# Gate and up tiles as seven block products, and a new order in the state-space stage

## The chip, the cores and the metric

The kernel runs on one core of a Trainium2 chip. The metric is the device time of one execution in microseconds. TensorE (PE) multiplies matrices and loads their weights (PEld) beside it, VectorE (DVE), ScalarE (ACT) and GpSimd (POOL) do the elementwise work, and SyncE (SP) issues nearly all transfers. Each engine runs its instructions in the order in which they stand, and waits on semaphores for the others. Products are summed in PSUM, eight banks of 512 float32 columns on 128 partitions; everything else lies in SBUF.

## The reference

The model is a trunk of two layers on 512 tokens of width 1024. Layer 0 mixes tokens with a diagonal state-space model, a gated projection (GLU) and an output projection; layer 1 with stick-breaking attention of 16 heads. After each mixer comes a feed-forward block of hidden width 2816, and after each of the four parts a normalisation of the scaled input plus the part's output.

```python
def swiglu_ffn(x, w_gu, w_down):
    g, u = jnp.split(x @ w_gu, 2, axis=-1)
    return (jax.nn.silu(g) * u) @ w_down
...
    for i in range(DEPTH):
        ...
        h = layer_norm(DEEPNORM_ALPHA * h + mix, ln_mix_g[i], ln_mix_b[i])
        h = layer_norm(DEEPNORM_ALPHA * h + swiglu_ffn(h, ffn_w_gu[i], ffn_w_down[i]),
                       ln_ffn_g[i], ln_ffn_b[i])
```

## The kernel before

Every float32 operand of a large product is split into a rounded high part and a low part that holds the rest, and a product is three passes: high by high, low weights by high, high weights by low (`mm3`). x lies transposed in `xh` and `xl`, 8 blocks of 128 features by 512 tokens. A weight chunk is 128 x 1024: it is brought in by SP as `raw`, ACT copies its high part `wh`, and DVE (or POOL, where `l_eng` says so) subtracts to get `wl` (`Weights.pump`, lines 228 and 231). All such tiles come from one ring of 37 SBUF slots that are handed out in the order in which they came free, so a transfer can wait for the last reader of its slot.

The feed-forward block (`ffn`) has 22 tiles of 128 hidden features. A tile is one gate chunk and one up chunk, 8 blocks x 3 passes x 2 = 48 matmuls of 512 columns (`fm`, lines 292 to 294), then SiLU on ACT (L409), the product with up on DVE (L410), and the split of the result (L287, L288). Tiles 0 and 1 are made by `ffn_first` at the end of the mixer, first for tokens 0 to 255 and then for the rest, so that PE has work while the last two of four token tiles are normalised (`ln`, L332 to L345) and transposed (`tr`, L357). The down product follows: 22 chunks into all eight banks for the first 14, and the last 8 token tile by token tile (`tail`), so that normalisation can start early.

In both feed-forward blocks DVE works in the order in which the code is written, in the second one ACT too; elsewhere a scheduler orders the instructions. The state-space stage follows a string, `SSM_ORDER`: each letter is a piece of work for one of four blocks of groups (g, j, h and i make tables on DVE, t and T transpose, m, k and y are small matmuls, e is a table on POOL, r and s rotate and scan, z applies GELU, l splits its result, n fetches a Toeplitz matrix from a DRAM scratch by 16 transfers), `d9` is nine unused matmuls of two passes that keep PE's clock up, `u1` is one item of GLU work on finished blocks, `p` and `q` split the next weight chunk with POOL or DVE, `a` adds partial GLU sums on POOL. `GLU_FIRST` lists those items: a GLU tile and the quarters of its input features; what isn't listed follows behind the stage.

## Time and profile before

| | us |
|---|---|
| median of 3 runs | 1248.2 (1247.43 to 1248.39) |
| profiled execution | 1248.96 |
| its span | 1247.2 |
| PE busy | 1191.5 |
| DVE busy | 666.4 |
| ACT busy | 422.6 |
| POOL busy | 190.5 |

A row of a time line gives start, length, engine, line, operation, tiles and shapes, and in brackets the engine's idle time before it and what ended it. A row of instruction groups gives count, total busy time, mean length in ns, and the idle time before them with its causes. A window row gives length and then, engine by engine, busy time and number of instructions (PE, PEld, DVE, ACT, POOL), the clock that TensorE was granted, the share of the transfer engines in use, and GB/s. Matmuls overlap, so that a row's length is more than the time to the next row's start.

### The profile page before, as it was taken

What the parts mean: (1) busy time and instruction counts of PE and PEld (TensorE: products, weight loads), DVE (VectorE), ACT (ScalarE), POOL (GpSimd) and SP (SyncE); (2) the same over time, 40 slices, a digit from 0 to 9 for tenths busy, and PEclk for the clock granted to TensorE, in tenths of its full rate; (3) what the DMA queues carried; (4) which work ended last, traced back from release to release, by engine and by line L of the source; (5) the groups of instructions that cost most, each with busy time, mean ns of one, the idle gap of its engine ahead of it and who ended that gap; (6) DMA issues with size and microseconds to landing.
All of it is one profiled execution on the core that took longest, in us unless ns stands there. A gap on an engine that the chain in (4) does not pass through costs nothing.

```text
span 1247.2 us, 16906 instructions
## 1 busy us (share of the span) xinstructions
PE 1191.5 (96%) x6964; PEld 989.7 (79%) x6964; DVE 666.4 (53%) x1033; ACT 422.6 (34%) x601; POOL 190.5 (15%) x212
## 2 busy tenths in 40 slices
PE   3799999999999999999999999999999999999996
PEld 2577688898888888888887888878888888888885
DVE  8975666643323333234867787868433333333236
ACT  1355263142222222222246666653222223332200
POOL 6636302120000000001312222224200000000000
PEclk9899999999999999999999999999999999999998
DMA  5333453142222223442201122133322222234301
GB/s 192 111 94 92 144 195 112 37 149 69 85 85 85 85 84 106 148 136 84 85 7 63 52 68 62 58 101 122 133 85 85 85 85 85 69 117 152 102 17 51
DMA packets 44781, 117.66 MB, mean 94 GB/s; under 512 B 6816, under 2 KB 18080, under 8 KB 44576
## 3 DMA queue, kind: packets, MB, share of 16 engines
q1 hardware_dynamic: 44704, 116.59, 29.3%
q8 instruction: 54, 0.88, 0.3%
q14 instruction: 23, 0.19, 0.1%
HBM read 112.51 MB, written 4.06 MB: 93 GB/s over the span
## 4 chain that ended last, share of the span: by engine, by line
PE 83%; DVE 9%; ACT 3%; POOL 2%; issue 1%; DMA 1%; SPq 1%; DVEq 0%; POOLq 0%; ACTq 0%
PE psum L294 17%; PE psum L292 17%; PE psum L293 16%; PE psum L313 8%; PE psum L312 8%; PE psum L311 8%; PE psum L776 2%; DVE nb L1015 2%; PE psum L1037 1%; DVE h L466 1%; ACT wh L228 1%; DVE wl L231 1%; PE psum L1102 1%; PE psum L1053 1%; PE psum L687 1%
## 5 line engine op out<-in xcount | busy, mean ns | idle before, releaser
L292 PE MATMUL psum<-xh,wh 128*128 128x512 f32 (+1 forms) x1056 | 394.6, 374 | 0.8 <-ACT xh L287 0.8
L294 PE MATMUL psum<-xl,wh 128*128 128x512 f32 (+1 forms) x1056 | 393.6, 374 | 0.0
L293 PE MATMUL psum<-xh,wl 128*128 128x512 f32 (+1 forms) x1056 | 391.9, 372 | 0.0
L228 ACT ACTIVATE wh<-raw 128x1024 fp32r<-128x1024 f32 x188 | 194.5, 1055 | 228.4 <-PE psum L313 68.5
L231 DVE TENSOR_TENSOR wl<-raw,wh 128x1024 fp32r<-128x1024 f32 x158 | 196.7, 1274 | 131.7 <-ACT wh L228 103.8
L292 PEld LDWEIGHTS psum<-xh,wh 128*128 128x128 f32 x1056 | 198.4, 188 | 38.7 <-issue 3.0
L293 PEld LDWEIGHTS psum<-xh,wl 128*128 128x128 f32 x1056 | 198.4, 188 | 35.4
L294 PEld LDWEIGHTS psum<-xl,wh 128*128 128x128 f32 x1056 | 197.9, 188 | 33.5
L410 DVE TENSOR_TENSOR s<-s,psum 128x512 f32<-128x512 f32 x44 | 30.3, 688 | 278.9 <-PE psum L294 278.9
L231 POOL TENSOR_TENSOR wl<-raw,wh 128x1024 fp32r<-128x1024 f32 x30 | 74.1, 2485 | 512.6 <-DMA raw<-w_v 317.2
L313 PE MATMUL psum<-wh,hid 128*128 128x512 f32 x352 | 137.6, 391 | 0.0
L312 PE MATMUL psum<-wl,hid 128*128 128x512 f32 x352 | 137.4, 390 | 0.0
L311 PE MATMUL psum<-wh,hid 128*128 128x512 f32 x352 | 137.3, 390 | 0.0
L287 ACT ACTIVATE hid<-s 128x512 fp32r<-128x512 f32 x44 | 27.7, 629 | 172.4 <-DVE s L410 172.4
L313 PEld LDWEIGHTS psum<-wh,hid 128*128 128x128 f32 x352 | 66.1, 188 | 14.2
L312 PEld LDWEIGHTS psum<-wl,hid 128*128 128x128 f32 x352 | 66.1, 188 | 14.0
L311 PEld LDWEIGHTS psum<-wh,hid 128*128 128x128 f32 x352 | 66.1, 188 | 13.5
L1016 POOL TENSOR_TENSOR be<-be,nb 128x768 f32<-128x768 f32 (+1 forms) x24 | 49.5, 2062 | 98.2 <-DVE nb L1015 70.9
L1015 DVE TENSOR_TENSOR_SCAN nb<-nb,dm 128x384 f32<-128x384 f32 (+1 forms) x48 | 50.2, 1088 | 9.7 <-ACT nb L1010 6.9
L409 ACT ACTIVATE s<-psum 128x512 f32<-128x512 f32 x44 | 26.2, 596 | 76.9 <-PE psum L294 76.8
L288 DVE TENSOR_TENSOR hid<-s,hid 128x512 fp32r<-128x512 f32 x44 | 30.5, 693 | 31.9 <-ACT hid L287 31.9
L287 ACT ACTIVATE xh<-psum 128x512 fp32r<-128x512 f32 x24 | 14.0, 596 | 97.1 <-PE psum L357 93.7
(181 smaller groups left out, 1399.8 us busy)
## 6 DMA issues: line engine op xcount, KB each, us to landing
raw<-w_gu SPq DMA_DIRECT2D x88, 512.0 KB, 3.6
raw<-w_down SPq DMA_DIRECT2D x44, 512.0 KB, 3.6
raw<-w_glu SPq DMA_DIRECT2D x16, 512.0 KB, 4.5
raw<-w_qk SPq DMA_DIRECT2D x16, 512.0 KB, 3.6
raw<-w_out SPq DMA_DIRECT2D x8, 512.0 KB, 3.7
raw<-w_v SPq DMA_DIRECT2D x8, 512.0 KB, 3.6
raw<-w_o SPq DMA_DIRECT2D x8, 512.0 KB, 3.6
xres<-xs SPq DMA_DIRECT2D x4, 512.0 KB, 6.9
```

The source lines that it names most:

```text
L228: nc.scalar.activation(h, w, AF.Copy)
L231: (self.l_eng or nc.vector).tensor_tensor(out=l, in0=w, in1=h.bitcast(F32), op=SUB)
L287: self.nc.scalar.activation(h, src, AF.Copy)
L288: self.nc.vector.tensor_tensor(out=l, in0=src, in1=h.bitcast(F32), op=SUB)
L292: mm(out=out, lhsT=sh, rhs=mh, start=first, stop=False)
L293: mm(out=out, lhsT=sl, rhs=mh, start=False, stop=False)
L294: mm(out=out, lhsT=sh, rhs=ml, start=False, stop=last)
L311: mm(out=o, lhsT=sh[:, ts], rhs=hl[0][:, c], start=first, stop=False)
L312: mm(out=o, lhsT=sh[:, ts], rhs=hl[1][:, c], start=False, stop=False)
L313: mm(out=o, lhsT=sl[:, ts], rhs=hl[0][:, c], start=False, stop=last)
L1015: V.tensor_tensor_scan(nb[:, h], nb[:, h], dm[u], 0.0, MUL, ADD)
L1016: G_.tensor_tensor(out=be, in0=be, in1=nb, op=MUL)
```

## The change

From the third tile on, gate and up of one tile are taken as a 2 x 2 block product: rows gate and up, inner halves of 512 features, columns tokens 0 to 255 and 256 to 511. With G1, G2, U1, U2 as the weight blocks and X11, X12, X21, X22 as blocks of x (first index the feature half), seven products replace eight: G1 X11, G2 X21, S4 X22, U2 T4, S1 T1, S2 T2 and S3 T3, with S1 = U1 + U2, S2 = S1 - G1, S3 = G1 - U1, S4 = G2 - S2, and T1 = X12 - X11, T2 = X22 - T1, T3 = X22 - X12, T4 = X21 - T2. `split_pair` makes the sums S of the next tile in three steps between the products of the present one, s1 and s2 in PSUM banks 6 and 7, the two halves of `s` in SBUF, and splits everything; `pair` issues the products and adds them up; `x_forms` makes the four T once for each layer at the end of the mixer. The hidden tile stays whole in `hid` and is split later, in the down part (`take`). The first two down chunks are brought in and split within the last tile, and their products begin with the banks that this tile leaves free. Weights of such a tile come as two transfers together. At the end of the first feed-forward block two instead of three chunks are fetched ahead. In the state-space stage the order and the GLU items change (17 instead of 20 quarters in the stage), seven `d9` stand instead of two, and the second half of the first Toeplitz matrix is fetched through ACT's queue.

The core of the difference:

```diff
 GLU_FIRST, GLU_LAST = glu_items(
-    "30 50 10 40 60 20 51 41 31 001 112 212 7012 612")
+    "30 50 10 40 60 20 001 51 41 312 7012 612")
...
 SSM_ORDER = (
-    "x c0 e0 g0 j0 t0 h0 T0 b0 i0 m0 M0 k0 n0 d9 r0 d9 s0 B0 c1 p e1 y0 g1 z0 t1 j1 T1 m1 M1 h1 p l0 u1 i1 c2 e2 p "
-    "u1 k1 n1 r1 u1 p u1 u1 s1 g2 y1 t2 j2 z1 T2 m2 M2 h2 p u1 i2 c3 l1 p k2 n2 r2 u1 u1 u1 a p e3 s2 g3 y2 t3 j3 "
-    "z2 T3 m3 M3 h3 p u1 i3 p l2 k3 n3 r3 u1 u1 p s3 q y3 q w0 z3 a w4 l3 q q q"
+    "x c0 e0 g0 j0 t0 T0 d9 h0 b0 i0 m0 M0 k0 n0 d9 d9 r0 d9 d9 d9 d9 s0 B0 c1 p e1 y0 g1 t1 j1 T1 z0 m1 M1 h1 l0 "
+    "u1 i1 c2 p u1 k1 n1 p r1 u1 u1 u1 e2 s1 p g2 y1 j2 t2 T2 z1 m2 M2 h2 p i2 c3 k2 n2 u1 e3 r2 l1 p u1 u1 s2 y2 "
+    "g3 t3 j3 T3 z2 m3 M3 h3 i3 k3 p n3 u1 l2 r3 u1 s3 p q y3 q w0 z3 a w4 l3 q q q"
...
-            t = self.ring.get("raw", F32)
-            self.nc.sync.dma_start(out=t, in_=self.src[self.loaded])
+            src = self.src[self.loaded]
+            if self.loaded > self.split + 1 and any(isinstance(s, tuple) for s in self.src[self.split:self.loaded + 1]):
+                break
+            if isinstance(src, tuple):
+                if self.hold:
+                    break
+                t = [self.ring.get("raw", F32) for _ in src]
+                for a, b in zip(t, src):
+                    self.nc.sync.dma_start(out=a, in_=b)
+            else:
+                t = self.ring.get("raw", F32)
+                self.nc.sync.dma_start(out=t, in_=src)
             self.raw[self.loaded] = t
             self.loaded += 1
+    def split_pair(self, i, g, u):
...
+        s1, s2 = self.sums
+        gh, gl, bh, bl, c, sh, sl = tiles = [get("wf") for _ in range(7)]
+        a = [(gh[:, lo], gl[:, lo]), (gh[:, hi], gl[:, hi]), (sh[:, hi], sl[:, hi]), (bh[:, lo], bl[:, lo]),
+             (bh[:, hi], bl[:, hi]), (c[:, lo], c[:, hi]), (sh[:, lo], sl[:, lo])]
+        self.hl[i] = dict(tiles=tiles, a=a)
+        s = get("ws", F32)
+        tt(s[:, lo], g[:, lo], u[:, lo], SUB, G_)
+        nc.scalar.activation(gh, g, AF.Copy)
+        nc.scalar.activation(bh[:, lo], u[:, hi], AF.Copy)
+        tt(gl, g, f(gh), SUB, G_)
+        tt(bl[:, lo], u[:, hi], f(bh[:, lo]), SUB, G_)
+        yield
+        tt(s1, u[:, lo], u[:, hi], ADD)
+        tt(s2, s1, g[:, lo])
+        tt(s[:, hi], g[:, hi], s2)
+        nc.scalar.activation(bh[:, hi], s1, AF.Copy)
+        nc.scalar.activation(c[:, lo], s2, AF.Copy)
+        nc.scalar.activation(sh, s, AF.Copy)
+        tt(bl[:, hi], s1, f(bh[:, hi]))
+        tt(c[:, hi], s2, f(c[:, lo]))
+        yield
+        tt(sl, s, f(sh))
+        self.ring.put(g, u, s)
+        self.split += 1
+        self.load(i + 1)
+    def begin(self, i):
+        if i >= len(self.src) or not isinstance(self.src[i], tuple):
+            return iter(())
+        self.load(i)
+        return self.split_pair(i, *self.raw.pop(i))
...
-        self.c_gu[l] = [[ws.add(io["w_gu"][l, i, v]) for v in range(2)] for i in range(KF)]
+        self.c_gu[l] = [[ws.add(io["w_gu"][l, i, v]) for v in range(2)] for i in range(2)]
+        self.c_gu[l] += [ws.add((io["w_gu"][l, i, 0], io["w_gu"][l, i, 1])) for i in range(2, KF)]
...
+    def x_forms(self, t):
...
+        x1, x2 = k4(u[:, :512]), k4(u[:, 512:])
+        part = lambda i, src: self.split(self.xf[i][0][:, :, c], self.xf[i][1][:, :, c], src)
+        tt(x1, x(self.xh, ka), x(self.xl, ka), ADD)
+        tt(x2, x(self.xh, kb), x(self.xl, kb), ADD)
+        yield
+        tt(u1, p1, x1)
+        tt(p2, p2, u1)
+        tt(x1, p2, x1)
+        tt(x2, x2, p2)
+        yield
+        part(1, p2)
+        part(0, u1)
+        part(2, x1)
+        part(3, x2)
+        ring.put(u, v)
+    def pair(self, i, a, ahead):
...
+        x11, x21, x22 = x(slice(0, 4), lo), x(slice(4, 8), lo), x(slice(4, 8), hi)
+        t1, t2, t3, t4 = self.xf
+        a11, a12, s4, a22, s1, s2, s3 = a
+        two = lambda t: t.rearrange("p (a b) -> p a b", a=2)
+        cu, vy = self.cv[:, 0:S], self.cv[:, S:2 * S]
+        s = self.tmp.tile([128, S], F32, tag="s", name="s")
+        def product(b, w, x):
+            wh, wl = (t.rearrange("p (k m) -> p k m", k=4) for t in w)
+            for k in range(4):
+                self.mm3(P[:, b], wh[:, k], wl[:, k], x[0][:, k], x[1][:, k], k == 0, k == 3)
+        next(ahead, None)
+        product(0, a11, x11)
+        p1 = vy[:, lo]
+        nc.scalar.activation(p1, P[:, 0], AF.Copy)
+        product(2, a12, x21)
+        product(3, s2, t2)
+        tt(two(cu), p1.unsqueeze(1).to_broadcast([128, 2, 256]), P[:, 2:4])
+        nc.scalar.activation(s[:, lo], cu[:, lo], AF.Silu)
+        next(ahead, None)
+        product(4, s1, t1)
+        product(5, s3, t3)
+        tt(two(vy), two(cu)[:, 1:2].to_broadcast([128, 2, 256]), P[:, 4:6])
+        tt(P[:, 5], vy[:, lo], P[:, 5])
+        next(ahead, None)
+        product(2, s4, x22)
+        product(3, a22, t4)
+        tt(P[:, 2:4], two(vy), P[:, 2:4])
+        nc.scalar.activation(s[:, hi], P[:, 2], AF.Silu)
+        o = self.hidden(i)
+        tt(two(o), two(s), P[:, 3:6:2], MUL)
...
-            store(3)
+            if forms:
+                E = mybir.EngineType
+                f, g = self.x_forms(2), self.x_forms(3)
+                next(f)
+                next(g)
+                with self.tc.manual_schedule(engines={E.Activation, E.DVE}):
+                    next(f)
+                    self.tr(3)
+                    next(g)
+                    for h in (f, g):
+                        for _ in h:
+                            pass
+            else:
+                store(3)
...
         for i in range(KF):
-            b = 2 * (i % 4)
             if i > 1:
-                for v in range(2):
-                    c = self.c_gu[l][i][v]
-                    hl = ws.get(c)
-                    for _ in self.fm(self.ps[:, b + v], hl):
-                        pass
-                    ws.done(c)
-            s = self.tmp.tile([128, S], F32, tag="s", name="s")
-            nc.scalar.activation(s, self.ps[:, b], AF.Silu)
-            nc.vector.tensor_tensor(out=s, in0=s, in1=self.ps[:, b + 1], op=MUL)
-            t = ring.get("hid")
-            self.split(t[:, 0:S], t[:, S:2 * S], s)
-            hid.append(t)
+                c = self.c_gu[l][i]
+                if i == 2:
+                    self.cv = ring.get("cv", F32)
+                E = mybir.EngineType
+                with self.tc.manual_schedule(engines={E.PE, E.DVE} | ({E.Activation} if i == KF - 1 else set())):
+                    a = ws.get(c, 0)["a"]
+                    self.pair(i, a, ws.begin(c + 1) if i < KF - 1 else ahead())
+                ws.done(c)
+            else:
+                b = 2 * i
+                s = self.tmp.tile([128, S], F32, tag="s", name="s")
+                nc.scalar.activation(s, self.ps[:, b], AF.Silu)
+                nc.vector.tensor_tensor(out=self.hidden(i), in0=s, in1=self.ps[:, b + 1], op=MUL)
+        ring.put(self.cv, *self.xf_tiles)
...
         for k in range(KF - nres):
             c = self.c_dn[l][k]
-            hl = ws.get(c)
-            for t in (2, 3, 0, 1):
-                self.tm(t, hl, *part(k), k == 0, False)
-            ws.done(c)
-            ring.put(hid[k])
+            ws.get(c)
+            take(k + (k // 2 if k > 4 else 1))
+            for t, j in ((), ((3, 0), (0, 0), (3, 1), (0, 1), (1, 0), (2, 0), (1, 1), (2, 1)))[k] if k < 2 else (
+                    (t, k) for t in (2, 3, 0, 1)):
+                self.tm(t, ws.hl[self.c_dn[l][j]], *part(j), j == 0, False)
+            for j in ((), (0, 1))[k] if k < 2 else (k,):
+                ws.done(self.c_dn[l][j])
+                ring.put(hid[j])
+        take(KF)
...
+        ws.nraw = 2
         self.tail(tiles, nxt, out)
+        ws.nraw = 3
...
-                self.ws.pump(self.c_gu[l][1][1] + 3 + i)
+                self.ws.hold = False
+                self.ws.pump(self.c_gu[l][2])
...
-                    nc.sync.dma_start(out=tn[hf][n * 16:(n + 1) * 16].rearrange("p (g t) -> p g t", g=8),
-                                      in_=kd[b, hf * 8:hf * 8 + 8, 0:16, n * 16:n * 16 + 128].rearrange("g h t -> h g t"))
+                    (nc.scalar if b == 0 and hf else nc.sync).dma_start(
+                        out=tn[hf][n * 16:(n + 1) * 16].rearrange("p (g t) -> p g t", g=8),
+                        in_=kd[b, hf * 8:hf * 8 + 8, 0:16, n * 16:n * 16 + 128].rearrange("g h t -> h g t"))```

On three places of the engines' queues the change reads as follows. First DVE in the gate/up stage of the first layer: one tile before (`s` is SiLU of gate, then the product; `wl` are low parts of weights for a later tile), and one tile now (`raw_3277` and `raw_3278` are gate and up of the next tile, `ws` is its `s`, `wf` the split weights, `cv` the partial sums cu and vy).

```order
L410 TENSOR_TENSOR s<-s,psum 128x512
L288 TENSOR_TENSOR hid_2936<-s,hid_2936 128x512
L231 TENSOR_TENSOR wl_2940<-raw_2841,wh_2939 128x1024
L231 TENSOR_TENSOR wl_2970<-raw_2877,wh_2969 128x1024
L410 TENSOR_TENSOR s<-s,psum 128x512
```

```order
L453 TENSOR_TENSOR cv_2696<-cv_2696,psum 128x512
L233 TENSOR_TENSOR psum<-raw_3278 128x512
L233 TENSOR_TENSOR psum<-psum,raw_3277 128x512
L233 TENSOR_TENSOR ws_3320<-raw_3277,psum 128x512
L233 TENSOR_TENSOR wf_3316<-psum,wf_3315 128x512
L233 TENSOR_TENSOR wf_3317<-psum,wf_3317 128x512
L453 TENSOR_TENSOR cv_2696<-cv_2696,psum 128x512
L453 TENSOR_TENSOR psum<-cv_2696,psum 128x256
L233 TENSOR_TENSOR wf_3319<-ws_3320,wf_3318 128x1024
L453 TENSOR_TENSOR psum<-cv_2696,psum 128x512
L453 TENSOR_TENSOR hid_3307<-s,psum 128x512
```

Four operations of a tile become eleven; only the second and the ninth of them read SBUF alone. Next ACT in the second layer, where it keeps the written order: one tile before, and one now (L244 copies the high part gh of the next tile's gate chunk, L245 that of half its up chunk, L472 takes the first product out of PSUM, L476 and L486 are SiLU of the two token halves, L252 to L254 copy the high parts of the sums).

```order
L409 ACTIVATE s<-psum 128x512
L287 ACTIVATE hid_7640<-s 128x512
L228 ACTIVATE wh_7643<-raw_7545 128x1024
L228 ACTIVATE wh_7673<-raw_7581 128x1024
L409 ACTIVATE s<-psum 128x512
```

```order
L486 ACTIVATE s<-psum 128x256
L244 ACTIVATE wf_9629<-raw_9593 128x1024
L245 ACTIVATE wf_9631<-raw_9594 128x512
L472 ACTIVATE cv_8767<-psum 128x256
L476 ACTIVATE s<-cv_8767 128x256
L252 ACTIVATE wf_9631<-psum 128x512
L253 ACTIVATE wf_9633<-psum 128x512
L254 ACTIVATE wf_9634<-ws_9636 128x1024
L486 ACTIVATE s<-psum 128x256
```

The copies for the next tile stand behind the second SiLU of the tile before and ahead of the present tile's first partial sum. Last, DVE at the end of the first mixer, from the last normalisation step of token tile 3 on: before, and now (`xl` is the low part of transposed x, `u` and `v` hold the T in the making, `xf` their low parts).

```order
L345 SCALAR_TENSOR_TENSOR xres<-xres,rq_y,lnb_1733 128x512 x2
L288 TENSOR_TENSOR xl<-psum,xh 128x4x128 x4
L410 TENSOR_TENSOR s<-s,psum 128x512
L288 TENSOR_TENSOR hid_2612<-s,hid_2612 128x512
L410 TENSOR_TENSOR s<-s,psum 128x512
```

```order
L403 SCALAR_TENSOR_TENSOR xres<-xres,rq_y,lnb_1722 128x512 x2
L346 TENSOR_TENSOR xl<-psum,xh 128x4x128 x2
L422 TENSOR_TENSOR v_2515<-psum,u_2514 128x512
L422 TENSOR_TENSOR psum<-psum,v_2515 128x512
L422 TENSOR_TENSOR u_2514<-psum,u_2514 128x512
L422 TENSOR_TENSOR u_2514<-u_2514,psum 128x512
L346 TENSOR_TENSOR xl<-psum,xh 128x4x128 x2
L422 TENSOR_TENSOR v_2519<-psum,u_2518 128x512
L422 TENSOR_TENSOR psum<-psum,v_2519 128x512
L233 TENSOR_TENSOR psum<-raw_2562 128x512
L422 TENSOR_TENSOR u_2518<-psum,u_2518 128x512
```

The two low parts of token tile 3 stood right behind those of tile 2; four operations come between them now, and sixteen more follow before the first hidden product.

69 lines of the change are left out of this document (61 added, 8 removed).

## Prediction

> **What bounds the kernel now.** I read the page's engine totals and its chain of waits first, then the time line of one gate/up tile, then that of the two places around the feed-forward halves where TensorE (PE) changes work.
>
> ```profile
> span 1247.2 us, 16906 instructions
> PE 1191.5 (96%) x6964; PEld 989.7 (79%) x6964; DVE 666.4 (53%) x1033; ACT 422.6 (34%) x601; POOL 190.5 (15%) x212
> PE 83%; DVE 9%; ACT 3%; POOL 2%; issue 1%; DMA 1%; SPq 1%; DVEq 0%; POOLq 0%; ACTq 0%
> ```
>
> PE is busy for 1191.5 of 1247.2 us and holds 83% of the chain. At most 56 us can be won by waiting less; more than that needs less matmul time. In the gate/up stage VectorE (DVE) shows the rhythm, because each tile ends with its product of gate and up:
>
> ```profile
> 305.55 0.69 DVE L410 TENSOR_TENSOR s<-s,psum 128x512 f32<-128x512 f32 x1 [6.43 <-PE psum L294]
> 306.99 0.69 DVE L288 TENSOR_TENSOR hid<-s,hid 128x512 fp32r<-128x512 f32 x1 [0.75 <-ACT hid L287]
> ...
> 316.54 0.69 DVE L410 TENSOR_TENSOR s<-s,psum 128x512 f32<-128x512 f32 x1 [6.58 <-PE psum L294]
> ...
> 327.52 0.69 DVE L410 TENSOR_TENSOR s<-s,psum 128x512 f32<-128x512 f32 x1 [6.63 <-PE psum L294]
> 300.00:310.00 10.00, 10.00 (x45) 8.22 (x44) 3.65 (x4) 2.97 (x5) 0.00 (x0) 1.00 0.23 87
> ```
>
> One tile takes (327.52 - 305.55)/2 = 10.98 us, and each time DVE has waited 6.4 to 6.6 us for PE. In the window row PE fills all 10.00 us at the full clock (1.00), DVE 3.65, ACT 2.97, POOL nothing. So this stage is PE alone: 48 matmuls of 512 columns in 10.98 us, 0.2288 us each.
>
> **The change, part by part.** *Matmul time of a tile.* The new tile has seven products of 4 blocks and 3 passes, 84 matmuls of 256 columns. The same shape with the same kind of weights stands in the trace, at the start of the first two gate/up tiles:
>
> ```profile
> 247.38 0.28 PE L292 MATMUL psum<-xh,wh 128*128 128x256 f32 x1
> ...
> 252.81 0.28 PE L293 MATMUL psum<-xh,wl 128*128 128x256 f32 x1
> L292 PEld LDWEIGHTS psum<-xh,wh 128*128 128x128 f32 x1056 | 198.4, 188 | 38.7 <-issue 3.0
> ```
>
> Between these two rows are 46 steps: 5.43/46 = 0.118 us. The difference to 0.2288 us is 0.1108 us for 256 columns, so only 0.007 us of a matmul doesn't scale with columns. A tile costs PE 84 x 0.118 = 9.91 us, 1.07 us less than 10.98, though columns fall by an eighth: the 36 extra matmuls give a quarter microsecond back. That is at most 40 x 1.07 = 42.8 us in two layers. A load of weights lasts 188 ns, longer than the 118 ns in which the next matmul follows, so the loads already overlap here. The Trainium skill (TensorE: Matmul & The Clock Gate, The mechanism) says that a weight load overlaps running matmuls only if it goes to other rows of the array, which speaks against any change that makes more and shorter matmuls; the trace disagrees with 0.118 us, and what the rule would make of the time is a rival below.
>
> *Vector work of a tile.* It is now the second candidate, with these rows:
>
> ```profile
> L231 DVE TENSOR_TENSOR wl<-raw,wh 128x1024 fp32r<-128x1024 f32 x158 | 196.7, 1274 | 131.7 <-ACT wh L228 103.8 <-PE psum L313 22.0 <-POOL be L1016 3.2
> L231 POOL TENSOR_TENSOR wl<-raw,wh 128x1024 fp32r<-128x1024 f32 x30 | 74.1, 2485 | 512.6 <-DMA raw<-w_v 317.2 <-ACT wh L228 148.5 <-PE psum L294 46.6
> L466 POOL TENSOR_TENSOR e<-e,eu 128x512 f32<-128x512 f32 x8 | 10.1, 1283 | 0.0
> L228 ACT ACTIVATE wh<-raw 128x1024 fp32r<-128x1024 f32 x188 | 194.5, 1055 | 228.4 <-PE psum L313 68.5 <-PE psum L293 38.8 <-PE psum L312 33.5
> L287 ACT ACTIVATE w<-psum 128x256 fp32r<-128x256 f32 x80 | 29.2, 382 | 33.7 <-DVE w L288 20.7 <-PE psum L1037 12.4 <-DVE oT L288 0.2
> ```
>
> DVE per tile, in the order of the change: nine operations of 512 columns at 0.69 (cu, s1, s2, the upper half of s, two low parts, vy, the last sums, the final product), one of 256 (0.42 by the 0.69 and half its columns) and the 1024-wide low part sl at 1.22: 7.85 us, against 0.69 + 0.69 + 2 x 1.2 = 3.8 before. The final product also waits for the second SiLU, 0.38 us plus two hand-overs; these cost 0.12 us together (306.99 - 305.55 = 0.69 + 0.63 + 0.12). So DVE needs 8.35 us of PE's 9.91 if nothing else stops it. POOL gets the low part of the gate tile and two halves, 2.49 + 1.28 + 1.28 = 5.0 us. ACT has 1.06 x 2, 0.6 x 3 and 0.38 x 3, about 5.1 us. No engine is over PE's time, but DVE has 1.5 us left, and here is what can take them:
>
> ```profile
> 238.59 0.74 DVE L342 SCALAR_TENSOR_TENSOR xres<-xres,mv,lng 128x512 f32<-128x512 f32 x1
> 249.40 2.13 DVE L342 SCALAR_TENSOR_TENSOR xres<-xres,mv,lng 128x512 f32<-128x512 f32 x1
> 251.58 2.76 DVE L342 SCALAR_TENSOR_TENSOR xres<-xres,mv,lng 128x512 f32<-128x512 f32 x1
> 246.20 10.39 POOL L231 TENSOR_TENSOR wl<-raw,wh 128x1024 fp32r<-128x1024 f32 x4 [37.15 <-ACT wh L228]
> ```
>
> The same DVE operation takes 0.74 us while POOL is idle, and 2.13 and 2.76 us while four POOL subtractions of 2.6 us run: with two inputs in SBUF it waits until POOL's present instruction is through. Of the new DVE operations only s1 and sl have both inputs in SBUF; the others read PSUM, like L410.
>
> In the first layer a scheduler orders ACT and puts the copy gh of a tile two tiles ahead behind the first SiLU; POOL's long subtraction then begins after s1 is done, and only sl meets one of POOL's short ones. That costs one wait of up to 1.28 us and, where gh stands ahead of a copy that DVE needs, up to 1.06 us. The second wait shifts DVE's phase once and doesn't return each tile. I take 10.0 us (bounds 9.91 and 10.6): 20 x 0.98 = 19.6 us won.
>
> In the second layer ACT keeps the written order, and this closes a ring: second SiLU, gh of the next tile (1.06), its low part on POOL (2.49), s1 behind it (0.69), s2, half of s, two low parts and vy (5 x 0.69), 0.42, sl (1.22), the last sums (0.69), SiLU again (0.38): 10.4 us. The hand-overs add some 0.2 us, and independent operations follow each other after 0.61 instead of 0.69 us, which takes as much away. This is over 9.91. Bounds: 9.91 if s1 gets in before POOL, 12.1 if sl has to wait too. I take 10.4: 20 x 0.58 = 11.6 us won.
>
> The transfers are not in it: two take the place of two before, 3.6 us each from issue to landing, and their places come free two tiles before they are split.
>
> ```profile
> raw<-w_gu SPq DMA_DIRECT2D x88, 512.0 KB, 3.6
> raw<-w_down SPq DMA_DIRECT2D x44, 512.0 KB, 3.6
> ```
>
> *The ends of the two mixers.* Here the new forms of x are made, where PE is covered by 96 short matmuls and barely so:
>
> ```profile
> 247.59 0.75 DVE L332 SCALAR_TENSOR_TENSOR xres<-xres,psum 128x256 f32<-128x256 f32 x2 [2.90 <-PE psum L313]
> ...
> 260.87 1.29 DVE L288 TENSOR_TENSOR xl<-psum,xh 128x512 fp32r<-128x512 f32 x2 [0.76 <-ACT xh L287]
> 260.89 0.39 PE L292 MATMUL psum<-xh,wh 128*128 128x256 f32 x1 [0.25 <-ACT xh L287]
> ```
>
> PE waits 0.25 us for tile 3 of the normalised x. Now four SBUF additions (2.8 us) stand in the gap of 2.90 us, and POOL starts inside it (246.20): the last of them can lose up to 2.5 us. POOL goes on with the first two weight pairs, so that the last two steps of the normalisation meet it too. Four PSUM operations (2.8 us) come between the normalisation and the low part of tile 3. Bounds 1 and 8 us a layer; I take 4.5, near the middle since POOL is busy about half of that time: 9 us lost. The eight splits behind them end about when tile 2's third product needs them.
>
> *Down.* The hidden splits (0.63 on ACT, 0.69 on DVE) move into a stage where a step of 24 matmuls lasts 24 x 0.2288 = 5.5 us and DVE needs 1.22 + 1.5 x 0.69 = 2.3: hidden. The first down parts use banks that the last pair doesn't hold. Before, PE had no wait there either. Zero; without that cover 22 x 0.69 = 15 us a layer would stand in the way.
>
> *The state-space stage.*
>
> ```profile
> 31.31 4.29 PE L660 MATMUL psum<-ident 128*128 128x128 f32 x36
> 40.11 0.70 PE L776 MATMUL psum<-xl,xres 128*64 128x128 f32 x4 [4.51 <-DMA xl<-kd]
> 40.00:45.00 5.00, 4.89 (x36) 3.07 (x36) 4.33 (x14) 0.30 (x2) 0.51 (x2) 0.50 0.79 208
> DVE h L466 <- POOL e L466: 7.8, 1, 7.8
> sum 170.00, PE 132.27 PEld 104.19 DVE 124.18 ACT 64.68 POOL 85.57; mean PE 3.89 PEld 3.06 DVE 3.65 ACT 1.90 POOL 2.52
> ```
>
> The last row adds the 5 us windows from 0 to 170. PE idles 37.7 us in these, most of it before 40.11, where DVE sets the pace. Two groups of fill matmuls last 4.29 us; six stand ahead of the first y now, 12.9 us from 31.3 to 44.2, later than 40.11 by 4 us, but the clock then isn't 0.50. The additions on POOL that held back DVE for 7.8 us move to the end. Three of 20 quarters of the gate product move behind the stage, where PE does them at the same price. Bounds 6 us won and 6 lost; I take 2 won.
>
> **Sum.** The profiled execution took 1248.96 us (span 1247.2 and 1.8 around it): 1248.96 - 19.6 - 11.6 + 9 - 2 = 1224.8. The median of the runs shown lies 0.8 us lower: **1224 us**.
>
> **The rivals.** *PE sets the pace in both layers:* DVE's 8.35 us fit, s1 slips in before POOL. Then 42.8 won, 9 lost, 2 won: 1212 us. For it: POOL is free half of the time; against it: the ring of 10.4.
> *DVE behind POOL sets it in both:* s1 waits for a whole long subtraction (2.49) and sl for a short one (1.28) in every tile: 8.35 + 3.8 = 12.1 us, 40 x 1.1 = 45 us lost, with the other terms 1300 us. It is slower than before from 10.8 us a tile on, since 40 x 0.18 = 7 us is what the other terms cost. For it: 2.13 and 2.76 us above; against it: once DVE is late, POOL has finished by then.
> *The gain is eaten at the ends:* 8 us lost at each mixer's end, 6 in the state-space stage, and 10.5 us a tile: 1248 - 19 + 22 = 1251 us; with 10.3 a tile, 1243.
> *Weight loads aren't hidden* in the new pattern: then a matmul can't follow faster than a load of 0.188 us, a tile takes 84 x 0.188 = 15.8 us, and the time is over 1400 us. Only the skill's rule speaks for it.
>
> **How the numbers follow.** Chances: ring in layer two alone 0.42, PE in both 0.32, gain eaten 0.12, DVE behind POOL in both 0.12, loads 0.02. The likeliest one's own range is 1215 to 1234. The range 1205 to 1247 takes in PE in both and half of the eaten gain, and leaves out most of the two slow cases and a state-space stage that wins all of its bound. A measurement of this kernel can't tell less than 0.2% (2.5 us) from no change. Faster by more: 0.42 + 0.32 + two thirds of 0.12 = 0.82; within: 0.03; slower: 0.15.
>
> **What would show it.** DVE's final product of a tile should come every 9.9 to 10.1 us in the first feed-forward half and every 10.3 to 10.6 in the second, with PE waiting there for DVE or ACT and s1 lasting well over 0.69 us next to a POOL subtraction. PE's wait for tile 3 of x should grow from 0.25 to some 4 us, and the matmuls of 256 columns should follow each other after 0.118 us. The end of the state-space stage should differ by under 6 us once three quarters of gate work are counted. I am wrong if s1 and sl wait in every tile of both layers, if PE waits at the first down part, or if a tile waits for a transfer.

## The result and the profile after

The changed kernel takes 1218.3 us (median of 4 runs, 1218.1 to 1223.0) against 1248.2 us: ratio 0.9771, 95% interval 0.9747 to 0.9795. A second set of runs, described below, gave 0.9765 (0.9750 to 0.9780). The page of the profiled execution (1223.0 us, the longest of the four; the other three lie at 1218.1 to 1218.3):

```profile
span 1221.3 us, 20799 instructions
PE 1164.6 (95%) x8494; PEld 1041.3 (85%) x8494; DVE 897.0 (73%) x1403; ACT 512.1 (42%) x813; POOL 383.4 (31%) x320
PE 83%; DVE 7%; DMA 2%; ACT 2%; issue 1%; POOL 1%; SPq 0%; DVEq 0%; POOLq 0%; ACTq 0%
```

PE still holds 83% of the chain. It has lost 26.9 us of busy time, about the 25.9 us by which the span is shorter; DVE has gained 231 us and POOL 193 us, and almost all of that lies beside PE. The two stretches of block products, from the first final product of a tile to the first down part, as windows (length, then PE, PEld, DVE, ACT, POOL, granted clock, transfers), and the group of the final products in each (min/median/max ns, start of the first and of the last):

```profile
290.70:478.20 187.50, 187.50 (x1575) 187.50 (x1574) 149.25 (x206) 89.19 (x150) 91.11 (x51) 1.00 0.33 112
903.30:1091.60 188.30, 188.30 (x1582) 188.30 (x1581) 149.51 (x206) 87.98 (x150) 97.59 (x53) 1.00 0.32 110
```

```profile
L453 DVE TENSOR_TENSOR hid<-s,psum x20: 686/687/689, 290.7 to 480.2; 128x512 f32<-128x512 f32 x20
L453 DVE TENSOR_TENSOR hid<-s,psum x20: 686/689/691, 903.3 to 1093.7; 128x512 f32<-128x512 f32 x20
```

A matmul of 256 columns takes 187.50/1575 = 0.119 us, weight loads are under way all the time, and DVE is busy for 80% of it. A tile takes (480.2 - 290.7)/19 = 9.97 us in the first feed-forward half and 10.02 us in the second, where the kernel before took 10.98. These are means: in the first half single tiles end 8.5 to 11.1 us apart; in the second all but two come after 9.95 to 10.13 us, one after 11.14 and the last after 8.25. That is 20 x 1.01 + 20 x 0.96 = 39.4 us won. The span shows 25.9 of them. By marks on PE:

| stretch | before | after | difference |
|---|---|---|---|
| start to the first 256-column gate matmul of layer one | 247.38 | 250.37 | +3.0 |
| from there to the first down part | 244.67 | 227.80 | -16.9 |
| down part, attention, to the first gate matmul of layer two | 378.85 | 381.86 | +3.0 |
| from there to the first down part | 246.59 | 231.57 | -15.0 |
| rest | 129.71 | 129.70 | 0.0 |

The two feed-forward stretches give back 20.2 - 16.9 = 3.3 and 19.2 - 15.0 = 4.2 us: these are the ends of the mixers. Three us are lost up to the end of the first mixer, but only in this execution (a second profile, shown below, has this mark at 246.8), and three in the stretch with the attention, whose code is unchanged. The experiments take these apart: first the length of a tile, then the ends, then the attention, then the state-space stage.

### The profile page after: what moved, and what is told of

It reads as the page before. It is cut to its first block, busy times and chain, and to the rows that moved or that the text cites. A ratio compares the mean times of both kernels' runs of the same rounds, so it can differ in the third digit from the quotient of the medians.

```text
span 1221.3 us, 20799 instructions
## 1 busy us (share of the span) xinstructions
PE 1164.6 (95%) x8494; PEld 1041.3 (85%) x8494; DVE 897.0 (73%) x1403; ACT 512.1 (42%) x813; POOL 383.4 (31%) x320
## 4 chain that ended last, share of the span: by engine, by line
PE 83%; DVE 7%; DMA 2%; ACT 2%; issue 1%; POOL 1%; SPq 0%; DVEq 0%; POOLq 0%; ACTq 0%
PE psum L350 16%; PE psum L352 15%; PE psum L351 15%; PE psum L370 9%; PE psum L371 9%; PE psum L369 9%; PE psum L957 3%; DVE nb L1196 1%; PE psum L1218 1%; PE psum L1283 1%; DVE wl L286 1%; PE psum L1285 1%; PE psum L1284 1%; ACT wh L283 1%; PE psum L415 1%
## 5 line engine op out<-in xcount | busy, mean ns | idle before, releaser
L233 POOL TENSOR_TENSOR wf<-raw,wf 128x1024 fp32r<-128x1024 f32 (+1 forms) x80 | 161.2, 2031 | 217.0 <-ACT wf L244 96.4
L351 PE MATMUL psum<-xf,wf 128*128 128x256 f32 x640 | 181.1, 283 | 0.6 <-DVE wf L233 0.6
L352 PE MATMUL psum<-xf,wf 128*128 128x256 f32 x640 | 181.5, 284 | 0.0
L350 PE MATMUL psum<-xf,wf 128*128 128x256 f32 x640 | 181.2, 283 | 0.0
L286 DVE TENSOR_TENSOR wl<-raw,wh 128x1024 fp32r<-128x1024 f32 x88 | 116.8, 1338 | 64.3 <-ACT wh L283 45.6
L350 PE MATMUL psum<-xh,wh 128*128 128x512 f32 (+1 forms) x416 | 147.8, 356 | 1.8 <-ACT xh L980 1.3
L283 ACT ACTIVATE wh<-raw 128x1024 fp32r<-128x1024 f32 x108 | 112.3, 1053 | 81.4 <-PE psum L371 28.3
L352 PE MATMUL psum<-xl,wh 128*128 128x512 f32 (+1 forms) x416 | 142.3, 345 | 1.3 <-DVE xl L346 0.8
L351 PE MATMUL psum<-xh,wl 128*128 128x512 f32 (+1 forms) x416 | 142.1, 343 | 0.0
L371 PE MATMUL psum<-wh,hid 128*128 128x512 f32 x352 | 137.7, 391 | 0.0
L370 PE MATMUL psum<-wl,hid 128*128 128x512 f32 x352 | 137.4, 390 | 0.0
L350 PE MATMUL psum<-xh,wf 128*128 128x256 f32 x480 | 134.7, 281 | 0.5 <-DVE hid L585 0.5
L352 PE MATMUL psum<-xl,wf 128*128 128x256 f32 x480 | 133.9, 279 | 0.0
L351 PE MATMUL psum<-xh,wf 128*128 128x256 f32 x480 | 133.9, 279 | 0.0
L286 POOL TENSOR_TENSOR wl<-raw,wh 128x1024 fp32r<-128x1024 f32 x20 | 49.5, 2482 | 253.3 <-DVE wl L286 150.1
L351 PEld LDWEIGHTS psum<-xf,wf 128*128 128x128 f32 x640 | 122.2, 191 | 0.8 <-DVE wf L233 0.8
L350 PEld LDWEIGHTS psum<-xf,wf 128*128 128x128 f32 x640 | 122.6, 192 | 0.0
L352 PEld LDWEIGHTS psum<-xf,wf 128*128 128x128 f32 x640 | 122.2, 191 | 0.0
L350 PEld LDWEIGHTS psum<-xh,wf 128*128 128x128 f32 x480 | 90.4, 188 | 0.7 <-DVE hid L585 0.7
L453 DVE TENSOR_TENSOR cv<-cv,psum 128x512 f32<-128x512 f32 x80 | 54.6, 683 | 49.5 <-PE psum L352 43.3
L350 PEld LDWEIGHTS psum<-xh,wh 128*128 128x128 f32 x416 | 79.4, 191 | 12.7 <-issue 2.8
```

The costliest lines, as they stand in the source:

```text
L233: tt = lambda o, a, b, op=SUB, e=V: e.tensor_tensor(out=o, in0=a, in1=b, op=op)
L283: nc.scalar.activation(h, w, AF.Copy)
L286: (self.l_eng or nc.vector).tensor_tensor(out=l, in0=w, in1=h.bitcast(F32), op=SUB)
L350: mm(out=out, lhsT=sh, rhs=mh, start=first, stop=False)
L351: mm(out=out, lhsT=sl, rhs=mh, start=False, stop=False)
L352: mm(out=out, lhsT=sh, rhs=ml, start=False, stop=last)
```

## Experiments on the length of a tile

My prediction said that a ring through ACT, POOL and DVE sets 10.4 us a tile in layer two. The mean tile takes 10.02 us, so either there is no ring or it is shorter. One tile of layer two in the time line of the changed kernel (three engines, in order of time):

```profile
953.14 0.39 ACT L486 ACTIVATE s<-psum 128x256 f32<-128x256 f32 x1 [2.60 <-DVE psum L453]
953.43 1.05 ACT L244 ACTIVATE wf<-raw 128x1024 fp32r<-128x1024 f32 x1
954.56 4.11 POOL L233 TENSOR_TENSOR wf<-raw,wf 128x1024 fp32r<-128x1024 f32 x2 [0.68 <-ACT wf L244]
955.96 0.69 DVE L453 TENSOR_TENSOR cv<-cv,psum 128x512 f32<-128x512 f32 x1 [1.71 <-PE psum L352]
956.56 0.96 DVE L233 TENSOR_TENSOR psum<-raw 128x512 f32<-128x512 f32 x1
957.55 0.70 DVE L233 TENSOR_TENSOR psum<-psum,raw 128x512 f32<-128x512 f32 x1
958.29 0.69 DVE L233 TENSOR_TENSOR ws<-raw,psum 128x512 f32<-128x512 f32 x1
958.92 1.41 DVE L233 TENSOR_TENSOR wf<-psum,wf 128x512 fp32r<-128x512 f32 x2
960.25 0.68 DVE L453 TENSOR_TENSOR cv<-cv,psum 128x512 f32<-128x512 f32 x1
960.96 0.43 DVE L453 TENSOR_TENSOR psum<-cv,psum 128x256 f32<-128x256 f32 x1
961.30 1.22 DVE L233 TENSOR_TENSOR wf<-ws,wf 128x1024 fp32r<-128x1024 f32 x1
962.43 0.69 DVE L453 TENSOR_TENSOR psum<-cv,psum 128x512 f32<-128x512 f32 x1
963.16 0.39 ACT L486 ACTIVATE s<-psum 128x256 f32<-128x256 f32 x1 [2.60 <-DVE psum L453]
...
964.57 2.41 POOL L233 TENSOR_TENSOR wf<-raw,wf 128x1024 fp32r<-128x1024 f32 x1 [4.64 <-ACT wf L244]
```

The ring is there, and every link of it is tight: second SiLU (953.14), gate copy gh (953.43), POOL's low part right behind it (954.56; alone it takes 2.41 us, the last row, so it ends at 956.97), s1 on DVE, which starts at 956.56 but lasts 0.96 instead of 0.69 us and ends half a microsecond behind POOL's end, and then eight DVE operations without a gap to the next second SiLU at 963.16. It takes 10.02 us. But in the row of 955.96 DVE had waited 1.71 us for PE, and PE itself has no wait in this stretch. So ring and PE are equally long here, and the trace alone can't say which of them sets the pace, or whether it would matter. Making the ring longer can.

**The second sum twice.** s2 is computed a second time with the same result. It stands inside the ring and reads PSUM.

```diff
-        tt(s2, s1, g[:, lo])
+        tt(s2, s1, g[:, lo]); tt(s2, s1, g[:, lo])
```

> The changed kernel with the second sum of each weight pair (s2, 512 columns, PSUM) computed twice on the vector engine: 0.70 us more for it in each of 40 tiles, behind s1 and ahead of everything that leads to the second SiLU. Ring theory (in the second layer second SiLU, gate copy, POOL's low part, s1 ... second SiLU close a ring that is exactly as long as the tile): layer two takes 10.7 us a tile, 20 x 0.7 = 14 us more, layer one, where the gate copy isn't behind the second SiLU, nothing: 1232. PE theory (PE sets the pace, the vector engine has some 1.1 us to spare in both): at most 2 us more, 1218 to 1220. Third: the vector engine is full in both layers: 28 us more, 1246.

Measured: 1231.2 us (1230.4 to 1232.8), ratio to the kernel before 0.9869 (0.9847 to 0.9892). Final products in layer one and layer two, and PE's waits in layer two:

```profile
L453 DVE TENSOR_TENSOR hid<-s,psum x20: 686/687/691, 286.5 to 475.7; 128x512 f32<-128x512 f32 x20
L453 DVE TENSOR_TENSOR hid<-s,psum x20: 686/687/691, 900.0 to 1103.8; 128x512 f32<-128x512 f32 x20
```

```profile
PE psum L350 <- DVE cv L453: 9.7, 16, 1.9
```

9.96 us a tile in layer one, 10.73 in layer two: the added 0.70 us appears whole in layer two (10.02 + 0.70 = 10.72) and not at all in layer one, and PE, which waited for nothing there before, now waits for DVE 16 times, 0.6 us each. The ring theory said 1232 us.

**The same with the ring open.** The first phase of the next weight pair is written behind the first SiLU, so that gh is no longer behind the second one on ACT.

```diff
-        next(ahead, None)
         product(0, a11, x11)
...
         nc.scalar.activation(s[:, lo], cu[:, lo], AF.Silu)
-        next(ahead, None)
+        next(ahead, None); next(ahead, None)
```

> As the run with the sum done twice, and the first phase of the next weight pair (the copies of the gate tile and POOL's low parts) is written behind the first SiLU instead of ahead of the tile; this moves the gate copy in layer two on the scalar engine from behind the second SiLU to behind the first. Ring theory: the ring is open, POOL's low part no longer stands ahead of s1, and the 0.7 us are hidden: 1217 to 1221. If the 0.7 us were paid because the vector engine is full, they are paid here too: 1232 or more, with POOL's low part now next to sl.

Measured: 1219.4 us (1218.6 to 1222.7), ratio 0.9782 (0.9759 to 0.9805). Layer two is back at 9.94 us a tile with the doubled sum still in it, layer one at 10.03. So the 14 us of the run before were not DVE's work but its place in the ring. That settles that the ring exists, and that in the changed kernel it has no room left.

**The ring open, nothing added.**

> The changed kernel with only the first phase of the next weight pair written behind the first SiLU. The ring of layer two is open then, but it was no longer than the tile: ring theory: layer two from 10.02 to 9.94 us a tile (what the run with the doubled sum showed), layer one 9.97 to 10.03: 0 to 2 us won, 1216.5 to 1218.5. If the ring had cost the changed kernel the 0.4 us a tile that the prediction gave it, 8 us would be won: 1210.

Measured: 1218.1 us (1217.3 to 1222.3), ratio 0.9772 (0.9750 to 0.9793); tiles of 10.05 and 10.00 us. Opening the ring wins nothing that can be told from none in the unloaded kernel. The ring stood at PE's own pace, 84 x 0.119 = 10.0 us.

**How much DVE needs.** With the ring open, s2 is computed four times.

> The changed kernel with the gate copies behind the first SiLU (ring open) and the second sum done four times: 2.1 us more for the vector engine in each tile. The prediction counted 8.35 us of it a tile, so 10.45 now, over PE's 9.91: the tile should show the vector engine's own need. If the count is right and nothing else holds it: 10.45 to 10.6 us a tile, 40 x 0.5 = 20 us more than 1218: 1237 to 1243. If waits for POOL's instructions (1.28 to 2.5 us) come on top in every tile: 11.5 us or more, over 1275. If the count was too high by the 0.08 us between neighbours: 9.9 to 10.1, under 1225.

Measured: 1244.6 us (1241.9 to 1250.0), ratio 0.9971 (0.9954 to 0.9988): 26 us more. The added work is the same in both layers, but from the first gate matmul to the first down part layer two takes 5.3 us more than with the ring open alone (235.7 against 230.4), and layer one 22.0 (249.8 against 227.9). A tile takes 10.10 us in layer two and 11.07 in layer one. The groups for s1 and the 1024-wide low part sl, in layer one and then in layer two:

```profile
L233 DVE TENSOR_TENSOR wf<-ws,wf 128x1024 fp32r<-128x1024 f32 x18 | 27.9, 1551 | 0.0
L233 DVE TENSOR_TENSOR psum<-raw 128x512 f32<-128x512 f32 x18 | 17.1, 951 | 0.0
...
L233 DVE TENSOR_TENSOR wf<-ws,wf 128x1024 fp32r<-128x1024 f32 x18 | 21.9, 1219 | 0.0
L233 DVE TENSOR_TENSOR psum<-raw 128x512 f32<-128x512 f32 x18 | 12.5, 694 | 0.0
```

In layer two neither of them waits for POOL. All tiles but the last (8.39 us) come every 10.15 to 10.23 us there, 0.2 more than with the ring open alone. DVE has no gap left but the 0.45 us in which it waits for the second SiLU, and the list of PE's waits has none, so DVE now sets this pace by a little. It needs 10.2 - 3 x 0.73 = 8.0 us for the tile without the three sums, not the 8.35 that I counted: I had added lengths, and independent neighbours follow each other after 0.60 to 0.73 us. In layer one the two operations lose 0.6 us a tile to POOL, and PE waits for POOL's low parts (7.7 us in six waits), ACT's copies (1.9 us in three) and DVE (2.7 us). These are 12.3 of the 22 us; what the rest is was not separated. My expectation of 10.45 to 10.6 us fits neither layer.

## Experiments on the ends of the mixers and on the attention

At the end of the attention mixer, POOL begins with the first weight pair while DVE still normalises the last token tiles. PE's wait for the transposes there, before, and then the same place in the changed kernel:

```profile
875.59 0.66 PE L357 MATMUL psum<-ident,xres 128*128 128x128 f32 x4 [1.73 <-DVE xres L345]
```

```profile
865.99 1.75 POOL L233 TENSOR_TENSOR ws<-raw,raw 128x512 f32<-128x512 f32 x1
866.57 1.71 DVE L400 SCALAR_TENSOR_TENSOR xres<-xres,mv,lng 128x512 f32<-128x512 f32 x1
867.70 2.85 POOL L233 TENSOR_TENSOR wf<-raw,wf 128x1024 fp32r<-128x1024 f32 x1
868.33 2.76 DVE L400 SCALAR_TENSOR_TENSOR xres<-xres,mv,lng 128x512 f32<-128x512 f32 x1
...
876.99 1.97 PE L415 MATMUL psum<-ident,xres 128*128 128x128 f32 x8 [4.61 <-DVE xres L403]
```

Two steps of 0.74 us last 1.71 and 2.76 us, each to half a microsecond behind the end of a POOL instruction, and PE then waits 4.61 us for the result (1.73 us before). More is lost behind this wait: the granted clock is 0.50 from 877 to 881.3 us, and matmuls of 256 columns follow each other every 0.21 us there instead of 0.119, which costs about one microsecond more.

**The first pair late.** Its transfer is issued from ACT's queue behind the copies of x tile 3.

```diff
-        self.hold = True
+        self.hold, self.q = True, nc.sync
...
-                    self.nc.sync.dma_start(out=a, in_=b)
+                    self.q.dma_start(out=a, in_=b)
...
-                    self.tr(3)
+                    self.tr(3); ws.hold, ws.q = False, nc.scalar; ws.load(ws.loaded); ws.q = nc.sync
```

> The changed kernel with the transfer of the first weight pair of each layer issued from the scalar engine's queue behind its copies of x tile 3, so that POOL's first low parts start behind the normalisation. Theory A (the ends of the mixers lose their time because the last normalisation steps and additions wait for POOL's instructions): the two normalisation steps of tile 3 take 1.4 us again instead of 4.0 in layer one, and 0.74 each instead of 1.71 and 2.76 in layer two; 5.6 us won less up to 2 us a layer for a first tile that now waits for its weights: 1213 to 1217. Theory B (the vector engine's work on the forms sets these ends, whatever POOL does): 1217 to 1219. Theory C (the transfer lands too late): the first tile of each layer waits 3 us or more, 1219 to 1224.

Measured: 1217.9 us (1216.4 to 1219.8), ratio 0.9764 (0.9747 to 0.9781): no difference that can be told from the changed kernel. The same place in layer two:

```profile
861.91 0.74 DVE L400 SCALAR_TENSOR_TENSOR xres<-xres,mv,lng 128x512 f32<-128x512 f32 x1
862.70 0.74 DVE L400 SCALAR_TENSOR_TENSOR xres<-xres,mv,lng 128x512 f32<-128x512 f32 x1
...
878.20 4.56 POOL L233 TENSOR_TENSOR wf<-raw,wf 128x1024 fp32r<-128x1024 f32 x2
878.72 4.60 DVE L346 TENSOR_TENSOR xf<-u,xf 128x512 fp32r<-128x512 f32 x2
...
886.03 0.39 PE L350 MATMUL psum<-xh,wf 128*128 128x256 f32 x1 [2.83 <-DVE hid L585]
```

The time is theory B's, but the first half of theory A holds: both steps are at 0.74 us again, and PE's wait for the transposes is 0.2 us. Of the 4.4 us, 3.0 are these two steps; ahead of them DVE had also waited 1.35 us for a copy of ACT, which is gone too. But POOL's next two low parts (4.56 us) now meet the last two splits of the forms (4.60 instead of 1.29 us), which also have both inputs in SBUF, and the first tile waits 2.8 us for a DVE product that stands behind them. From the first gate matmul to the first down part, layer two takes 228.2 instead of 231.6 us, layer one 230.4 instead of 227.8, with a wait of 3.4 us for the same product and a granted clock of 0.51 and 0.63 in the four microseconds behind it (274 to 278 us). The loss moved; in layer two it became smaller, in layer one larger. The Trainium skill (SBUF — State Buffer, SBUF: two separate sides) describes such a lock between the two engines: who has it keeps it for the whole instruction. These rows agree, and so do the operations with one input in PSUM in the tile shown above, which keep their 0.69 to 0.70 us beside POOL (957.55 and 958.29).

**The attention.** The loss shows in one row of the list of PE's waits and two of the time line:

```profile
PE psum L370 <- DVE wl L286: 3.0, 1, 3.0
```

```profile
828.91 7.52 POOL L286 TENSOR_TENSOR wl<-raw,wh 128x1024 fp32r<-128x1024 f32 x3 [14.36 <-ACT wh L283]
...
834.26 3.25 DVE L286 TENSOR_TENSOR wl<-raw,wh 128x1024 fp32r<-128x1024 f32 x1
```

In the kernel before, POOL paused behind the second one, and DVE's low part of the last output chunk fell into the pause:

```profile
843.15 4.75 POOL L231 TENSOR_TENSOR wl<-raw,wh 128x1024 fp32r<-128x1024 f32 x2 [14.37 <-ACT wh L228]
848.49 1.23 DVE L231 TENSOR_TENSOR wl<-raw,wh 128x1024 fp32r<-128x1024 f32 x1
849.85 2.41 POOL L231 TENSOR_TENSOR wl<-raw,wh 128x1024 fp32r<-128x1024 f32 x1 [1.95 <-ACT wh L228]
```

Now POOL makes three low parts of gate and up weights in a row, and DVE's takes 3.25 instead of 1.23 us beside the third. PE waits for it, 2.3 us longer than before (3.0 against 0.7), and behind the wait the granted clock is 0.50 from 838 to 840 us and 0.89 from 840 to 842, which accounts for more; the two together are about the 3.0 us by which the stretch is longer. In the edited kernel this chunk is split one step earlier:

```diff
-                hl = ws.get(self.c_o[k], 1 if t == 0 and k < 4 else 0)
+                hl = ws.get(self.c_o[k], 1 if t == 0 and k < 4 or k == 6 else 0)
```

> The changed kernel with the split of the last chunk of the attention's output weights written one chunk earlier, ahead of the last head pair. Theory A (the 3.0 us that the attention lost in the changed kernel are one low part on the vector engine, 3.25 us instead of 1.23 beside POOL's third low part in a row, for which PE waits 3.0 us): 3 us won, 1215.3, and PE has no wait for wl there. Theory B (the stretch is set by the softmax of the last heads, the wait only moves): 1217.5 to 1218.5, with PE waiting for the output of the last heads instead.

Measured: 1215.8 us (1213.9 to 1217.3), ratio 0.9746 (0.9728 to 0.9763), 2.5 us under the changed kernel, nearly theory A. The intervals of the two ratios overlap, and the start of the execution varies by more (see below), so the marks tell more: from the first down part to the one of layer two it is 610.7 us, against 613.4 and 613.5 in the two profiles of the changed kernel. PE's longest waits from 780 to 880 us:

```profile
PE psum L415 <- DVE xres L403: 4.4, 2, 2.8
PE psum L371 <- DVE oT L346: 1.4, 1, 1.4
PE psum L1218 <- DVE w L346: 1.2, 1, 1.2
```

The wait for wl is gone. Two waits of 1.4 and 1.2 us on the last heads take its place, as theory B had it, and still 2.7 us are won. The first transposes come 370.9 us behind the first down part instead of 373.1. The scheduler also orders this stage differently now: ten more matmuls of the output projection stand ahead of the first gate matmul, and the wait at the last transposes is 2.8 instead of 4.6 us. So the low part beside POOL was the cause of its own wait, but what the edit wins comes in part from the new order.

**All three together.**

> The three edits together: gate copies behind the first SiLU, first pair's transfer late, last output chunk split early. If theory A holds for the latter two: 3 + 2 to 5.6 + 0 to 1.6 us won: 1208 to 1213. If B for both: 1216 to 1218.

Measured: 1218.8 us (1217.3 to 1220.3), ratio 0.9766 (0.9748 to 0.9784): theory B's number, and a miss for A. Layer one now takes 10.12 us a tile, and 230.6 us for its whole stretch, so what the late pair and the open ring cost there eats what the early split brings.

**The early split, and the late pair in layer two only.**

```diff
-                    self.tr(3)
+                    self.tr(3); ws.hold, ws.q = ws.hold and lag == 1, nc.scalar; ws.load(ws.loaded if lag > 1 else -1); ws.q = nc.sync
```

> The run with the early split of the last output chunk (1215.8), and the late transfer of the first weight pair in layer two alone, where the run with both layers late had won 3.4 us between the first matmul of the gate and the first down part (228.15 against 231.57) while layer one had lost 2.6. If the two gains add: 1212 to 1213. If the gain in layer two was the other order that came with the old attention end: 1215 to 1217.

The late pair now only follows `lag > 1`, which is the end of the attention mixer. Measured: 1215.4 us (1213.0 to 1216.1), ratio 0.9727 (0.9711 to 0.9743). The gains don't add: from the first gate matmul of layer two to its first down part it is 229.2 us, against 228.8 with the early split alone. The normalisation is through earlier, and from the first block product on it takes 204.3 instead of 200.3 us; 2.3 us of that are a wait of PE for a hidden product, as in the run with both pairs late. In the same set of runs the changed kernel took 1219.4 (1218.5 to 1220.3), so the edited one is 4.0 us faster with no overlap of their runs, and the fastest version here.

## Experiments on the state-space stage

**The new order alone**, in the kernel before: the two strings, the order of the gate's two halves, and the transfer of half a block's table from ACT's queue.

> The kernel before with only the state-space part of the change: the new order of its steps with six groups of fill matmuls, three fewer quarters of gate work in it, one half of a block's table fetched from the scalar engine's queue. Theory A (the prediction's term): 2 us won, 1246.2 against 1248.2. Theory B (the one profiled execution of the changed kernel, whose normalisation behind this stage starts 3.0 us later than before): 1251.2. Theory C (that execution was itself 4.8 us longer than the three others, and the excess lay in this stage): between 1245.5 and 1247.5, with the first y no longer at 46.5 us but nearer to 42.

Measured: 1246.0 us (1242.9 to 1248.4, 10 runs) against 1247.5 (1243.8 to 1250.9, 13 runs), ratio 0.9989 (0.9974 to 1.0004). The first y starts at 44.6 us and the first transposes of the normalised x at 218.0, against 40.1 and 221.1 in the kernel before. It is nearest to theory A's 2 us, and its interval still holds no change.

**The block products alone**, with the old order.

> The changed kernel with the old state-space order, that is the seven block products and the earlier down parts alone. By the booking of the two traces (tiles -39.6 us, ends of the two mixers +7.9, end of the attention +3.0) 28.7 us under the kernel before: 1219.5. If the state-space order brings 2 us, this kernel is at 1220.3, 2 us over the changed one (1218.3); if the state-space order costs 3 us, it is at 1215.3. Tiles should come every 9.97 and 10.02 us as in the changed kernel.

Measured: 1220.9 us (1215.6 to 1222.1), ratio 0.9781 (0.9752 to 0.9809); tiles of 10.02 us in both layers, and the attention's loss is there too (251.5 us between its first gate and the mixer's first transposes, as in the changed kernel, 248.4 before). So the block products carry the result, the 3.0 us in the attention come with them, and the state-space order adds 1 to 3 us (0.1% by the ratios, 2.5 us by the medians, which stem from different sets of runs); the intervals overlap, so that it adds anything is not shown.

**The changed kernel once more**, since its profiled execution was 4.8 us longer than the other three.

> The changed kernel itself once more. Its profiled execution took 4.8 us more than the three others. Theory A (late transfers of the state-space tables in that one execution): the first y starts at 44.5 to 46 us, when the six fill groups end, instead of 46.5 behind a transfer of 4.4 us; the first transposes of the normalised x come at 217.8 to 221 instead of 224.1; everything behind them within 0.3 us a stage of the first profile; 1218.3. Theory B (the excess lies in the feed-forward halves): the stages behind differ and the first transposes stay at 224.

Measured: 1219.4 us; the profiled execution has a span of 1216.8. The chain of waits at the first y, in the kernel before, in the changed kernel's first profile and in its second one:

```profile
40.12 10.06 PE psum L776 x96
```

```profile
41.92 4.37 DMA xl<-kd
46.54 7.72 PE psum L957 x96
```

```profile
33.41 12.26 PE psum L840 x108
45.67 7.65 PE psum L957 x96
```

In the second execution the six fill groups (12.26 us) end last before the first y; in the first one a transfer of 4.37 us did, at 46.3. That makes 0.9 us, and at 86.25 us, in the second y, both executions stand at the same matmul. The 3.6 us by which the first gate matmul is later in the first one (250.4 against 246.8) come at the last y, where PE waits for a table (first and second execution):

```profile
PE psum L957 <- DMA tn<-kd: 3.0, 1, 3.0
PE psum L957 <- DMA tn<-kd: 1.6, 1, 1.6
```

PE is 0.8 us late when this wait begins, waits 1.3 us longer, and then the y takes 9.15 instead of 7.68 us: in the windows 138 to 142 and 142 to 146 us the granted clock is 0.84 and 0.74, and 1.00 in the second execution. So theory A is right that a late table costs the time, but it is the last block's table and the lower clock behind the wait, not the first y. The other 0.9 us of the 4.5 lie in the first feed-forward half (227.8 against 226.9 us).

In the eleven profiles with the new order, the changed kernel's two among them, the first transposes come between 217.8 and 221.0 us, and once, in the changed kernel's first profile, at 224.1; with the old order they come at 221.1 and 220.7. So the same order in this stage ends up to 6 us apart from one execution to the next. The windows from 40 to 50 us of the kernel before and of the changed one (again) show what the fill matmuls do:

```profile
40.00:50.00 10.00, 9.89 (x96) 6.21 (x96) 9.00 (x19) 2.95 (x5) 4.19 (x5) 0.72 0.56 151
```

```profile
40.00:50.00 10.00, 10.00 (x107) 8.34 (x108) 9.00 (x20) 2.94 (x5) 4.03 (x5) 1.00 0.81 216
```

The granted clock is 1.00 instead of 0.72, and the first y takes 7.65 instead of 10.06 us; so of the 5.6 us by which it starts later, 2.4 come back at once.

## Why the prediction was right, and where it wasn't

The time, 1218.3, lies in the range and in the likeliest case's own range of 1215 to 1234; the forecast of 1224 was 6 us too high. That it came so close is in part luck: two terms were too pessimistic by 8.2 and 1.5 us, two others too hopeful by 3.0 and 0.5. By its terms:

- **256 columns in 0.118 us**: 0.119 measured, in windows where PE is busy throughout. The floor of 9.91 us a tile was right within 0.1 us, and the rival of weight loads that aren't hidden is out. By the sentence of the Trainium skill (TensorE: Matmul & The Clock Gate, The mechanism) that the prediction cites, one matmul every 0.188 us would have been the most; the same section also lets a load run ahead into a background weight buffer, and that fits these rows better: loads run throughout, one to each matmul.
- **Layer one, 10.0 us a tile**: 9.97. DVE's final product came every 9.97 us in the mean, but not every 9.9 to 10.1 as I had said: single tiles end 8.5 to 11.1 us apart, and PE has no wait all the same. s1 and sl do meet POOL. Their groups in layer one (count, busy time, mean ns) instead of 0.69 and 1.22 us each:

```profile
L233 DVE TENSOR_TENSOR wf<-ws,wf 128x1024 fp32r<-128x1024 f32 x18 | 27.2, 1510 | 0.0
...
L233 DVE TENSOR_TENSOR psum<-raw 128x512 f32<-128x512 f32 x18 | 17.4, 966 | 0.0
```

- **Layer two, 10.4 us a tile by a ring**: this is the step that failed, by its size. The ring exists link by link, and the run with the doubled sum shows that it is closed, but it is 10.02 us long. The 0.38 us are: copy behind SiLU 0.10 less than the sum of lengths, s1 done 0.55 instead of 0.69 us after POOL's end, 0.18 in the DVE operations that follow each other early, less 0.04 at the end. I had seen that neighbours follow after 0.61 us, and set it against hand-overs of 0.2; the rows show 0.08 us from ACT to POOL, which POOL's 2.41 instead of 2.49 us takes back, and the 0.04. It made 20 x 0.38 = 7.6 us, more than the whole error. The sign I gave for this case, PE waiting there for DVE or ACT, isn't seen either: PE has no wait. The case that I called "PE sets the pace in both layers" has the right tile, and its 1212 us missed by 6.3 us where my 1224 missed by 5.7.
- **The ends of the mixers, 9 us**: 3.3 + 4.2 = 7.5. The mechanism is the one named, steps with two SBUF inputs that wait for POOL. In layer two PE's wait grew from 1.73 to 4.61 us, and a granted clock of 0.50 behind it costs about one more, which the sum leaves out. The sign I gave, PE's wait for tile 3 of x, holds only in a small part: in layer two the wait stands one step earlier, at the transposes, and in layer one PE's waits grew from 0.25 to 2.1 us in four places (0.25 and 0.78 for tile 3 of x, 0.50 for a hidden product, 0.59 for a low part of the first weights). What makes the other 1.4 us of layer one was not followed.
- **The state-space stage, 2 us won**: 1.5 us alone (interval from 3.2 won to 0.5 lost). The fill groups delay the first y by 4.5 to 6.4 us in the three profiles read, where I had worked out 4, and the higher clock pays for 2.4 of it.
- **The attention**: not in the sum, 3.0 us lost. I had looked only at the stretches which the diff touches. It is the same lock, in a place where what changed is that POOL starts its third low part earlier; why it does was not followed.
- **Down**: 0.0 us, as said.

With the measured sizes, and the state-space stage as measured alone, the sum is 1248.96 - 39.4 + 7.5 + 3.0 - 1.5 = 1218.6 us. Against my 1224.8 the tiles bring 8.2 us more, the ends cost 1.5 less, the attention costs 3.0 more, and the state-space stage brings 0.5 less.

## What to carry to other kernels

Where an engine's order closes a ring over a loop, add up starts, not lengths, and then test it: do one operation of the ring twice and see in which layer the time appears; a ring that is just as long as the bound engine's work costs nothing today and everything that is added to it tomorrow. Work moved to POOL was paid for here by the next DVE operation with two SBUF inputs wherever PE waited for that, so look for one in every stretch where POOL's start may shift, also where the diff changes nothing, and expect a shifted start to move the loss before it removes it. More, shorter matmuls cost little here down to 256 columns: with 1.75 times the instructions a tile takes 10.0 us, where seven eighths of 10.98 would be 9.6. A wait of PE can cost more than its own length: behind the waits of 3.0, 3.0 and 4.6 us in the changed kernel the granted clock was 0.50 to 0.84 for some microseconds. Behind one of 1.6 us it stayed at 1.00, and behind one of 2.8 us it came out both ways (0.50 with the early split, 1.00 with the late pair in layer two), so no length from which on it happens follows from these runs.
